# Streaming conformer layer: VectorE's scalings by GpSimd's root, kept behind the VectorE instruction given just ahead of them

## The chip, the core and the metric

The kernel runs on one core of a Trainium2 chip. The metric is device time in microseconds for one launch, the median of several runs. A core has five engines with a queue of instructions each, issued in order: TensorE (matmuls and transposes, PE in the profile), VectorE (DVE), ScalarE (ACT), GpSimd (POOL) and SyncE (SP), whose queue here issues most DMA transfers. Engines wait for each other through semaphores.

## What is computed

One layer over 2048 prompt rows and 64 sample rows of width 1024, in float32:

```
h = rms_norm(x, norm1_g) * (1 + sc1) + sh1
z = h @ w_in
glu_a, glu_b, q, k, v, g_conv, g_attn = split(z)
u = glu_a * sigmoid(glu_b)
conv_out = silu(layer_norm(depthwise_conv31(hist, u) + b_dw)) @ w_conv_out
q = rms_norm(q.reshape(T, 8, 64), q_norm_g)
k = rms_norm(k.reshape(T, 8, 64), k_norm_g)
attn_out = band_attend(q, k, v, rel_bias) @ w_attn_out
x = x + gt1 * ((sigmoid(g_conv) * conv_out + sigmoid(g_attn) * attn_out) @ w_o)
h2 = rms_norm(x, norm2_g) * (1 + sc2) + sh2
x = x + gt2 * ((silu(gate) * up) @ w_ffn_out)
```

`sh1` to `gt2` come from a small product of a condition vector with `w_ada`; `gate` and `up` are the halves of `h2 @ w_ffn_in`. Each row attends to its own chunk of 64 and the eight before it. Returned are the rows, and the last rows of the convolution's input, of k and of v. What matters here are the three norms of the first part: each scales a row (or one head of it) by `1/sqrt(mean(x*x) + eps)`.

## The kernel before

**Stages.** The first part (to about 1,200 us) computes everything up to the mixers' outputs, in four blocks of token rows (576, then 512 each). Per block it runs eight stages: q, k and v, four convolution channel tiles (0 to 3), and the gates g. The second part joins the mixers and runs the feed-forward layers in three blocks. Matmul operands are split into a high and a low part (`whi`/`wlo`, `hh`/`hl`, `part_h`/`part_l`), and each product is three matmuls.

**Who sets the order.** The Python program gives instructions in one order. It keeps an estimate of each engine's load (`Stream`), and side work runs as generators in lanes: `norm_lane` (norms of the next block's rows), `work` (q and k rows), `attn` (attention heads), `tail` (layer norm of the convolution) and `conv` (convolution taps). A generator gives a few instructions, then yields a due time such as `stream.when("pool")`: GpSimd's estimated end less 200 ns. Between the matmuls of the main product, `Stream.tick` lets each lane go on whose due time is past. The framework then orders each engine's queue anew with a model of its own: an instruction that is ready there can go ahead of one that was given earlier and isn't. TensorE is excepted: from the end of the first block's q rows to the end of the first part its order is the given one (`tc.manual_schedule`). A block `with tc.issue_after(ins)` adds, to the instructions given in it on `ins`'s engine, an edge that keeps them behind `ins` in that engine's queue. The edge is order alone; no semaphore is added. The convolution's taps are already held so: each `scalar_tensor_tensor` in `convolve` stays behind the last entry of `ahead_of_taps`, which is the newest softmax step or, in the first block, the newest `t` of q and k rows.

**The norms.** `rsqrt_mean` has VectorE form `t = ssq/count + eps` and GpSimd raise it to the power −0.5 (`r<-t,mhalf` in the profile):

```
dve.tensor_scalar(t[:n, :width], ssq, 1.0 / count, EPS, ALU.mult, ALU.add)
stream.after("pool", "dve")
gps.tensor_tensor(r[:n, :width], t[:n, :width], mhalf[:n, :width], ALU.pow)
```

`qk_rows` runs 34 times, for 17 row tiles of q and 17 of k. ScalarE squares the product and copies it into `kn`; VectorE sums the squares (`ssq<-sq`) and forms `t`; GpSimd takes the root; then, once GpSimd's estimate is past, line 1087 scales `kn` (`kn<-kn,r`, 128x512). For k rows that are returned, a second product `ko<-kn,gk` follows and is stored. 5,000 estimated ns later `store_kq` transposes `kn` on TensorE (four transposes, `pt<-ident,kn`), splits the result on ScalarE (`part_h`) and VectorE (`part_l`) and stores both from SyncE's queue. `part_h` and `part_l` have two buffers each, shared with `conv_norm` and `finish_head`.

`norm_tile` runs 12 times, for the 4 row tiles of blocks 1 to 3. ScalarE sums squares in two halves, VectorE adds them and forms `t`, GpSimd takes the root, and line 1186 scales the rows (`x_t<-x_t,r`, 128x1024). Eight transposes on TensorE follow, in two groups with `h`, `hh` and `hl` made of each.

The first block's five row tiles are scaled elsewhere (`scale_rows`); the change doesn't touch them. The second part has norms of its own, scaled on ScalarE.

**Attention.** In a head, `softmax_max` reads a row tile's scores (`pr<-sc,bias`) on VectorE; the score matmuls of the next row tile (`sc<-kk,q`) wait for it. **Convolution.** `convolve` runs 31 taps over each channel tile, each reading and writing `y`, so that they are a chain on VectorE; for the returned rows it transposes the end of `u` first (`pt<-ident,u`).

Of the kernel before, what the change touches and what calls it, by code (L numbers as in the profile page):

```python
# [11 lines left out]
ALU = mybir.AluOpType  # L12
# [14 lines left out]
NH, HD = 8, 64  # L27
# [595 lines left out]
def streaming_layer(ctx: ExitStack, tc: tile.TileContext, I, O):  # L623
    nc = tc.nc
    stream = Stream()
    pe, dve, act, gps = (
        Meter(e, n, stream) for e, n in ((nc.tensor, "pe"), (nc.vector, "dve"), (nc.scalar, "act"), (nc.gpsimd, "pool"))
    )
# [106 lines left out]
    def either(n, less=0.0):  # L735

        d, p = (max(stream.load[e], stream.load["pe"]) for e in ("dve", "pool"))
        return (gps, "pool") if p + 60 + 2.25 * n + less < d + 75 + 1.04 * n else (dve, "dve")
# [7 lines left out]
    def rsqrt_mean(pool, ssq, n, width, count, bufs=5):  # L746
        t = pool.tile([P, 8], F32, tag="rs_t", bufs=bufs)
        r = pool.tile([P, 8], F32, tag="rs_r", bufs=bufs)
# [3 lines that stand above are left out]
        return r[:n, :width]  # L752
# [30 lines left out]
    def temp(name, shape=(P, 512)):  # L783
        return wk.tile(list(shape), F32, tag="t", name=name, bufs=NT)
# [138 lines left out]
    def first_block(xs):  # L923
# [87 lines left out]
        for i, (t, n) in enumerate(tiles):  # L1011
            for k in (KT - 2, KT - 1):
                product(i, k)
            work.start(qk_rows(pss[i], n, gqk[:, 0:1], q_d, t, None, i > 2))
# [23 lines left out]
    def store_kq(src, n, dst, col, g=None):  # L1038

        pt = ps_g.tile([P, 4, P], F32, tag="gp", name="pt")  # L1040
        for hp in range(4):
            pe.transpose(pt[:, hp, :n], src[:n, hp * P : (hp + 1) * P], ident[:n, :n])
        stream.after("act", "pe")
        hi, lo = parts(shape=(P, 4, P))
        if g is None:
            split(hi[:, :, :n], lo[:, :, :n], pt[:, :, :n])
        else:
            act.activation(hi[:, :, :n], pt[:, :, :n], AF.Copy, scale=g)
            stream.after("dve", "act")
            dve.scalar_tensor_tensor(lo[:, :, :n], pt[:, :, :n], g, hi[:, :, :n].bitcast(F32), ALU.mult, ALU.subtract)  # L1050

        def store():
            for j, t in enumerate((hi, lo)):
                nc.sync.dma_start(dst[j, :, :, col : col + n].rearrange("h p t -> p h t"), t[:, :, :n].bitcast(F32))

        stream.at(stream.when("act", "dve"), store)
# [12 lines left out]
    def qk_rows(ps, n, g, dst, col, out_rows, spare=False):  # L1069
        sq = temp("sq", (P, NH, HD))  # L1070
        ssq = wk.tile([P, NH], F32, tag="ssq8", bufs=5)
        if spare:
            kn = wa.tile([P, 2, NH, HD], F32, tag="x", name="kn", bufs=3)[:, 0]
        else:
            kn = wa.tile([P, NH, HD], F32, tag="kn", bufs=3)
        pv = ps[:n].rearrange("p (h d) -> p h d", h=NH)
        stream.after("act", "pe")
        act.activation(sq[:n], pv, AF.Square)
        act.activation(kn[:n], pv, AF.Copy)
        yield stream.when("act")  # L1080
        dve.tensor_reduce(ssq[:n], sq[:n], AX.X, ALU.add)
        r = rsqrt_mean(wk, ssq[:n], n, NH, HD)
        if col < PBLOCKS[0][1] + (dst is k_d) * CACHE:
            ahead_of_taps.append(dve.last.ins)
        yield stream.when("pool")
        e, name = either(512, TT_LESS)
        e.tensor_tensor(kn[:n], kn[:n], r.unsqueeze(2).to_broadcast([n, NH, HD]), ALU.mult)
        t = stream.when(name)
        if out_rows is not None:
            ko = temp("ko", (P, NH, HD))  # L1090
            e, name = either(512, TT_LESS)
            e.tensor_tensor(ko[:n], kn[:n], gk[:n].unsqueeze(1).to_broadcast([n, NH, HD]), ALU.mult)
            stream.at(stream.when(name), lambda: nc.sync.dma_start(out_rows, ko[:n].rearrange("p h d -> p (h d)")))
        yield t + KN_LAG
        store_kq(kn.rearrange("p h d -> p (h d)"), n, dst, col, g)
# [62 lines left out]
    def square(x_t, n, junk=None):  # L1158
        ssq = wk.tile([P, 2], F32, tag="ssq", name="ssq", bufs=3)
        if junk is not None:  # L1160
            act.activation(junk[:n], x_t[:n], AF.Square, accum_out=ssq[:n, 0:1])
            return rsqrt_mean(wk, ssq[:n, 0:1], n, 1, D)
        for j in range(2):
            act.activation(temp("junk")[:n], x_t[:n, 512 * j : 512 * j + 512], AF.Square, accum_out=ssq[:n, j : j + 1])
        stream.after("dve", "act")
        dve.tensor_tensor(ssq[:n, 0:1], ssq[:n, 0:1], ssq[:n, 1:2], ALU.add)
        return rsqrt_mean(wk, ssq[:n, 0:1], n, 1, D)
# [3 lines left out]
    def load_ahead():  # L1171

        if to_load:
            t = to_load.pop(0)
            ahead_x[t] = load_x(t, P, wa, "x", 3), stream.load["pe"] + X_LAG

    def norm_tile(lo, t, free):

        c = slice(t - lo, t - lo + P)
        while t not in ahead_x:  # L1180
            load_ahead()
        x_t, landed = ahead_x.pop(t)
        yield landed
        r = square(x_t, P)
        yield stream.when("pool")
        dve.tensor_scalar(x_t, x_t, r, None, ALU.mult)
        yield stream.when("dve") + PE_LAG
        for g in range(2):
            pt = ps_g.tile([P, 4, P], F32, tag="gp", name="pt")
            h = temp("h32", (P, 4, P))  # L1190
            for k in range(4):
                pe.transpose(pt[:, k], x_t[:, (4 * g + k) * P : (4 * g + k + 1) * P], ident)
            if g:
                stream.at(stream.when("pe"), load_ahead, True)
            stream.after("dve", "pe")
            for k in range(4):
                kk = 4 * g + k
                dve.tensor_scalar(h[:, k], pt[:, k], A1[:, kk, 0:1], B1[:, kk, 0:1], ALU.mult, ALU.add)
            yield stream.when("dve")
            yield lambda: free["columns"] >= c.stop  # L1200
            f = slice(4 * g, 4 * g + 4)
            act.activation(hh[:, f, c], h, AF.Copy)
            yield stream.when("act")
            dve.tensor_tensor(hl[:, f, c], h, hh[:, f, c].bitcast(F32), ALU.subtract)
    def qkv(b, m, norms):
        lo, hi = PBLOCKS[b]
        tiles = token_tiles(lo, hi)
        ws = {}

        def product(t, n, ps, k):  # L1210
            if k // 2 not in ws:
                ws[k // 2] = W.get(("qkv", m, k // 2))
            wh, wl = ws[k // 2]
            c = slice(t - lo, t - lo + n)
            mm3(ps[:n], hh[:, k, c], hl[:, k, c], wh[:, k % 2], wl[:, k % 2], k == 0, k == KT - 1)
            if (t, n) == tiles[-1] and k % 2:
                W.done()

        for t, n in tiles:
            if t in norms:  # L1220
                norm_lane.drain([norms[t]])
            ps = ps_g.tile([P, 512], F32, tag="gp", name="ps")
            for k in range(KT):
                product(t, n, ps, k)
            if m == 0:
                work.start(qk_rows(ps, n, gqk[:, 0:1], q_d, t, None))
            elif m == 1:
                work.start(qk_rows(ps, n, gqk[:, 1:2], k_d, kcol(t), state_row(ks_p, kn_s, t, n), b == 0 and t > 2 * P))
            else:
                v_rows(ps, n, t)  # L1230
# [415 lines left out]
    for b, stage in ORDER:  # L1646
        lo, hi = PBLOCKS[b]
        if stage == "q":
            free, ahead = {"columns": 0}, {}
            if b + 1 < len(PBLOCKS):  # L1650
                ahead = {t: norm_tile(hi, t, free) for t, _ in token_tiles(*PBLOCKS[b + 1])}
# [728 lines left out]
```

## Time and profile before

| | us |
|---|---|
| median of 3 runs (2952.1 to 2953.67) | 2952.1 |
| profiled execution | 2952.3 |
| its span on the core | 2950.5 |

How to read the profile: a group or a row gives the source line (nearly all have L105, a helper that gives every instruction), the engine, the operation, the written and read tiles with their shapes, and times. In rows in order of time the first number is the start, the second the duration in us, and a bracket at the end gives how long the engine stood idle before the instruction and what ended the wait. Rows of waits read: engine, tile it was about to write, what it waited for, then the sum, the number of times and the longest. PE's granted clock is a share of full speed.

| first part, by stage of time | TensorE busy | VectorE busy | GpSimd busy |
|---|---|---|---|
| 60 to 130 us | 68.34 of 70 | 54.18 | 19.09 |
| 340 to 372 us | 29.99 of 32 | 24.53 | 7.97 |
| 372 to 420 us | 42.30 of 48 | 34.98 | 7.76 |
| 940 to 982 us | 40.09 of 42 | 35.53 | 9.04 |
| 982 to 1230 us | 241.53 of 248 | 169.08 | 43.80 |

### The profile page before, as it was taken

How to read it: one execution, taken by the hardware profiler on the slowest of the kernel's cores; microseconds unless marked ns; L12 is line 12 of the kernel's file. 1: busy time of each engine (PE TensorE's matmuls, PEld its weight loads, DVE VectorE, ACT ScalarE, POOL GpSimd, SP SyncE). 2: the span in 40 equal slices, each digit the busy share in tenths (PEclk: the TensorE clock that was granted, in tenths of full speed). 3: DMA queues.
4: the chain of work that ended last, by engine and by line, in shares of the span. 5: the costliest groups of instructions: out<-in, count | busy, mean ns of one | idle time of the engine just before them, and what ended most of it. 6: DMA issues, size and time to landing. Idle time of an engine off the chain costs nothing.

```text
span 2950.5 us, 44832 instructions
## 1 busy us (share of the span) xinstructions
PE 2890.8 (98%) x16193; PEld 2585.3 (88%) x16193; DVE 2046.4 (69%) x3648; ACT 1363.3 (46%) x2453; POOL 1162.6 (39%) x753
## 2 busy tenths in 40 slices
PE   7999999999999999999999999999999999999999
PEld 5899777887888788888999998999999999999998
DVE  5897788667956885577767746666666557566666
ACT  3345533751465267464334345444444345444442
POOL 1101210111011002454566452366667742465667
PEclk9999999999999999999999999999999999999999
DMA  9989889978995997985444876332333965333333
GB/s 320 316 296 309 279 280 326 295 234 294 290 294 195 308 264 238 282 301 166 143 147 143 277 258 218 96 123 87 114 121 104 337 224 181 97 98 109 115 107 126
DMA packets 467067, 628.04 MB, mean 213 GB/s; under 512 B 36196, under 2 KB 314584, under 8 KB 466845
## 3 DMA queue, kind: packets, MB, share of 16 engines
q1 hardware_dynamic: 452944, 606.11, 63.6%
q10 hardware_dynamic: 13901, 19.08, 1.9%
q8 instruction: 127, 2.08, 0.3%
q14 instruction: 95, 0.78, 0.1%
HBM read 476.53 MB, written 148.54 MB: 212 GB/s over the span
## 4 chain that ended last, share of the span: by engine, by line
PE 46%; DVE 2%; DMA 1%; ACT 1%; issue 1%; POOL 0%; SPq 0%; ACTq 0%; DVEq 0%; POOLq 0%
PE ps L105 28%; PE pd L105 13%; PE pw L105 5%; DVE wlo L105 1%; ACT whi L105 0%; DVE ps L105 0%; DMA cin<-o_d 0%; DMA x<-x_d 0%; DMA wst<-in_w_conv_out 0%; POOL wlo L105 0%; DMA wfo<-in_w_ffn_out 0%; DVE acc L105 0%; DVE sums L105 0%; DVE pw L105 0%; DMA tg<-g_d 0%
## 5 line engine op out<-in xcount | busy, mean ns | idle before, releaser
L105 PE MATMUL ps<-t,whi 128*128 128x384 f32 (+1 forms) x2112 | 501.8, 322 | 3.2 <-DVE u L105 1.1
L105 POOL TENSOR_TENSOR wlo<-wst,whi 128x1024 fp32r<-128x1024 f32 (+1 forms) x159 | 363.4, 2297 | 235.0 <-ACT whi L105 213.6
L105 ACT ACTIVATE whi<-wst 128x1024 fp32r<-128x1024 f32 (+1 forms) x265 | 258.3, 979 | 317.0 <-PE ps L105 127.8
L105 PE MATMUL ps<-b,whi 128*128 128x384 f32 (+1 forms) x1584 | 380.6, 325 | 5.4 <-DVE v L105 2.1
L105 PEld LDWEIGHTS ps<-t,whi 128*128 128x128 f32 x2112 | 367.7, 188 | 10.5 <-ACT u L105 3.3
L105 DVE SCALAR_TENSOR_TENSOR y<-u,wd,y 128x512 f32<-128x512 f32 (+1 forms) x480 | 369.4, 773 | 7.2
L105 PE MATMUL ps<-hh,whi 128*128 128x512 f32 (+2 forms) x992 | 362.6, 365 | 0.1
L105 DVE TENSOR_TENSOR acc<-acc,pd 128x512 f32<-128x512 f32 x482 | 322.0, 684 | 48.4 <-PE pd L105 45.9
L105 PE MATMUL ps<-hh,wlo 128*128 128x512 f32 (+2 forms) x992 | 344.9, 348 | 0.0
L105 PE MATMUL ps<-hl,whi 128*128 128x512 f32 (+2 forms) x992 | 344.3, 347 | 0.0
L105 PE MATMUL ps<-t,wlo 128*128 128x384 f32 (+1 forms) x1056 | 338.2, 321 | 0.0
L105 PE MATMUL pd<-whi,hid 128*128 128x512 f32 x912 | 297.5, 391 | 0.5 <-DVE hid L105 0.3
L105 PEld LDWEIGHTS ps<-b,whi 128*128 128x128 f32 x1584 | 276.8, 188 | 13.6 <-DVE v L105 3.2
L105 ACT ACTIVATE pr<-pr,sm 128x640 f32<-128x640 f32 (+2 forms) x272 | 201.8, 748 | 138.5 <-DVE sm L105 136.6
L105 PE MATMUL ps<-b,wlo 128*128 128x384 f32 (+1 forms) x792 | 256.0, 323 | 0.0
L105 POOL TENSOR_TENSOR r<-t,mhalf 128x1 f32<-128x1 f32 (+2 forms) x68 | 82.3, 1219 | 415.5 <-DVE t L105 383.2
L105 PEld LDWEIGHTS ps<-hh,wlo 128*128 128x128 f32 x992 | 186.4, 188 | 22.7
L105 DVE TENSOR_TENSOR wlo<-wst,whi 128x1024 fp32r<-128x1024 f32 (+1 forms) x106 | 135.6, 1283 | 101.4 <-ACT whi L105 96.8
L105 PEld LDWEIGHTS pd<-whi,hid 128*128 128x128 f32 x912 | 171.1, 188 | 36.9 <-DVE acc L105 1.4
L105 PEld LDWEIGHTS ps<-hh,whi 128*128 128x128 f32 x992 | 187.0, 188 | 18.0 <-issue 2.9
L105 PEld LDWEIGHTS ps<-hl,whi 128*128 128x128 f32 x992 | 187.4, 189 | 14.5 <-issue 1.7
L105 PEld LDWEIGHTS ps<-t,wlo 128*128 128x128 f32 x1056 | 198.1, 188 | 0.8
(233 smaller groups left out, 6299.0 us busy)
## 6 DMA issues: line engine op xcount, KB each, us to landing
whi<-w_din_h SPq DMA_DIRECT2D x72, 512.0 KB, 6.9
wlo<-w_din_l SPq DMA_DIRECT2D x72, 512.0 KB, 7.0
wst<-sum_d SPq DMA_DIRECT2D x131, 256.0 KB, 2.9
wfo<-in_w_ffn_out SPq DMA_DIRECT2D x64, 512.0 KB, 4.1
wmod<-in_w_ada SPq DMA_DIRECT2D x46, 512.0 KB, 9.4
sum_d<-ws SPq DMA_DIRECT2D x88, 256.0 KB, 2.1
wst<-in_w_ffn_in SPq DMA_DIRECT2D x85, 256.0 KB, 3.3
wst<-in_w_in SPq DMA_DIRECT2D x40, 512.0 KB, 6.9
```

The lines of the kernel that those rows point to most:

```text
L105: self.last = f(*args, **kw)
```

## The change

The two scalings are put into a block that keeps them behind `dve.last.ins`, the VectorE instruction given last before them by any lane. Nothing else changes: the same instructions are given in the same order.

```diff
@@ qk_rows
         yield stream.when("pool")
         e, name = either(512, TT_LESS)
-        e.tensor_tensor(kn[:n], kn[:n], r.unsqueeze(2).to_broadcast([n, NH, HD]), ALU.mult)
+        with tc.issue_after(dve.last.ins):
+            e.tensor_tensor(kn[:n], kn[:n], r.unsqueeze(2).to_broadcast([n, NH, HD]), ALU.mult)
@@ norm_tile
         yield stream.when("pool")
-        dve.tensor_scalar(x_t, x_t, r, None, ALU.mult)
+        with tc.issue_after(dve.last.ins):
+            dve.tensor_scalar(x_t, x_t, r, None, ALU.mult)
```

`either(512, TT_LESS)` always chooses VectorE here, since `TT_LESS` is 9e9.

## The prediction

> **What bounds the kernel now.** I read the page's first and fifth parts, then the waits by engine, then the order in time around each scale.
>
> ```profile
> span 2950.5 us, 44832 instructions
> PE 2890.8 (98%) x16193; PEld 2585.3 (88%) x16193; DVE 2046.4 (69%) x3648; ACT 1363.3 (46%) x2453; POOL 1162.6 (39%) x753
> ```
>
> TensorE is busy 98% of the span, so only 59.7 us of it are idle, and the change touches no matmul. A change of VectorE's order can pay only where TensorE stands still for VectorE. The waits by engine say how much that is:
>
> ```profile
> DVE kn L105 <- POOL r L105: 33.4, 25, 3.9
> PE sc L105 <- DVE sm L105: 11.8, 9, 5.7
> ```
>
> VectorE waits 33.4 us in 25 places for GpSimd's root with a scale of `kn` at the head of its queue. TensorE's longest wait, 5.7 us, is that of a score matmul for VectorE's softmax. The first sum is about what VectorE can get back; what reaches the end is the part of it that stands in front of such TensorE waits.
>
> How a scale comes to wait, in VectorE's order in time:
>
> ```profile
> 948.90 0.15 DVE L105 TENSOR_SCALAR t<-ssq 128x8 f32<-128x8 f32 x1
> 949.01 0.75 DVE L105 SCALAR_TENSOR_TENSOR y<-u,wd,y 128x512 f32<-128x512 f32 x1
> 951.29 0.69 DVE L105 TENSOR_TENSOR kn<-kn,r 128x512 f32<-128x512 f32 x1 [1.53 <-POOL r L105]
> 949.20 2.05 POOL L105 TENSOR_TENSOR r<-t,mhalf 128x8 f32<-128x8 f32 x1 [5.87 <-DVE t L105]
> ```
>
> The root starts behind `t` and takes 2.05 us. One convolution tap (0.75) runs under it; then the scale heads the queue and VectorE stands for 1.53 us, though taps that need nothing from elsewhere are queued behind it.
>
> **The change, part by part.** Nothing is added or removed: the same 46 scales (34 of `kn`, 12 of `x_t`) run as long as before. Each may no longer be issued ahead of the VectorE instruction given last before it. By the order in which the kernel gives its instructions, set beside the order of the trace, 37 of the 46 now stand ahead of theirs, by 1 to 40 places; in nine the edge changes nothing. At 951.29 the instruction to be followed is a tap six places on. The root (2.05) is then covered by three taps of 0.75, and the 1.53 goes. What can be late instead is the scale's own reader, four transposes on TensorE, whose order in the first part is fixed by hand. The stores of q and k follow those transposes, so their DMAs on SyncE's queue move only if the transposes stall.
>
> (a) *The score wait at 387.* The order in time of VectorE, GpSimd and TensorE:
>
> ```profile
> 377.70 0.69 DVE L105 TENSOR_TENSOR kn<-kn,r 128x512 f32<-128x512 f32 x1 [0.60 <-POOL r L105]
> 382.21 0.69 DVE L105 TENSOR_TENSOR kn<-kn,r 128x512 f32<-128x512 f32 x1 [0.31 <-POOL r L105]
> 387.27 0.39 PE L105 MATMUL ps<-whi,hl 128*128 128x512 f32 x1
> 388.71 0.69 DVE L105 TENSOR_TENSOR kn<-kn,r 128x512 f32<-128x512 f32 x1 [1.53 <-POOL r L105]
> 389.98 0.68 DVE L105 TENSOR_TENSOR part_l<-o_p,part_h 128x512 fp32r<-128x512 f32 x1
> 393.02 0.27 DVE L105 CUSTOM_DVE_ANT_0 pr<-sc,bias 128x128 f32<-128x128 f32 x1
> 393.35 0.79 PE L105 MATMUL sc<-kk,q 128*128 128x256 f32 x2 [5.70 <-DVE sm L105]
> ```
>
> TensorE has nothing left at 387.66 and waits to 393.35 for the softmax step at 393.02. VectorE reaches that step late, having waited 0.60 + 0.31 + 1.53 = 2.44 us for roots. In the new order the scale of 382.21 comes behind the `part_l` of 389.98, still ahead of the step, and that of 388.71 behind a tap given after the step. Whether the place that it leaves is filled by another tap isn't known, so I count the stalls alone: 2.44. To it comes what the stretch before leaves VectorE ahead, bounded by 0 and 5.66 (the next rows); as VectorE waits there for TensorE and ScalarE too, I take 0.6. The score matmul starts 3.0 us earlier: **−3.0**, bounds 0 and −5.7 (no wait left).
>
> (b) *The stretch before it.*
>
> ```profile
> 346.15 0.69 DVE L105 TENSOR_TENSOR kn<-kn,r 128x512 f32<-128x512 f32 x1 [3.91 <-POOL r L105]
> 349.40 0.69 DVE L105 TENSOR_TENSOR kn<-kn,r 128x512 f32<-128x512 f32 x1 [1.75 <-POOL r L105]
> 355.90 0.51 PE L105 MATMUL sc<-kk,q 128*128 128x256 f32 x2 [0.95 <-DVE sm L105]
> 357.46 0.62 PE L105 MATMUL sc<-kk,q 128*128 128x384 f32 x2 [0.34 <-DVE sm L105]
> 360.67 0.60 PE L105 MATMUL pt<-ident,kn 128*128 128x128 f32 x4
> 366.11 0.74 DVE L105 SCALAR_TENSOR_TENSOR part_l<-pt,gqk,part_h 128x512 fp32r<-128x512 f32 x1
> 363.59 0.69 ACT L105 ACTIVATE part_h<-pt,gqk 128x512 fp32r<-128x512 f32 x1
> ```
>
> The scale of 346.15 has to follow the `part_l` of 366.11, 40 places on, which ends at 366.85. With 3.91 + 1.75 of waits gone and the later scale's 0.69 behind it too, the moved scale ends at 366.85 − 6.35 = 360.5 (its own 0.69 leaves its old place and comes back at the new one). TensorE, without its waits of 0.95 and 0.34, is at the transposes at 359.4: it waits 1.1 there and gets back 1.3. For the end this counts nothing, because the score matmul of (a) is set by VectorE: TensorE comes to it at 387.5 and goes on at 390.35, a wait of 2.9.
>
> (c) *The clock behind that wait.* Windows of VectorE's and TensorE's busy time (columns: PE, PEld, DVE, ACT, POOL busy and instructions; then granted clock, DMA share, GB/s):
>
> ```profile
> 306.79:310.20 3.41, 1.77 (x14) 1.77 (x15) 2.22 (x9) 1.25 (x5) 0.00 (x0) 1.00 0.69 183
> 388.71:392.12 3.41, 0.00 (x0) 0.00 (x0) 3.38 (x6) 0.22 (x1) 0.00 (x0) 1.00 0.65 205
> 392.12:395.53 3.41, 2.18 (x8) 1.89 (x8) 3.41 (x11) 1.30 (x4) 0.00 (x0) 0.50 0.93 269
> 402.00:410.00 8.00, 8.00 (x38) 6.50 (x37) 2.13 (x8) 3.39 (x8) 1.64 (x1) 0.98 1.07 342
> ```
>
> Behind the 3.41 us without a matmul the granted clock is 0.50, until about 402.3 (0.98 over the last row's 8 us leaves 0.3 us at half). From 393.35 that is 9.0 us of matmuls at half speed, 4.5 us lost. The other long wait, which falls into the first row, kept 1.00:
>
> ```profile
> 308.43 0.51 PE L105 MATMUL sc<-kk,q 128*128 128x256 f32 x2 [2.64 <-DVE sm L105]
> ```
>
> The 2.9 of (b) is nearer to 2.64 than to 5.70, so I take the clock as kept: **−4.5**, bounds 0 and −4.5. [...]
>
> (d) *The history transpose at 980.*
>
> ```profile
> 978.27 0.40 PE L105 MATMUL ps<-whi,hl 128*128 128x512 f32 x1
> 979.76 0.68 DVE L105 SCALAR_TENSOR_TENSOR u<-tb,ps 128x512 f32<-128x512 f32 x1
> 980.59 0.27 PE L105 MATMUL pt<-ident,u 128*30 128x128 f32 x1 [1.91 <-DVE u L105]
> ```
>
> VectorE starts `u` at 979.76 although its last input is there at 978.67, because taps are queued ahead. A stall of 1.53 at 951.29 goes in that stretch, and more like it, so the taps are through and `u` starts 1.0 earlier: **−1.0**, bounds 0 and −1.1.
>
> (e) *Late scales elsewhere.*
>
> ```profile
> 96.23 0.68 DVE L105 TENSOR_TENSOR kn<-kn,r 64x512 f32<-64x512 f32 x1 [1.53 <-POOL r L105]
> 102.29 0.69 DVE L105 TENSOR_TENSOR kn<-kn,r 128x512 f32<-128x512 f32 x1 [0.36 <-POOL r L105]
> 107.56 0.60 PE L105 MATMUL pt<-ident,kn 128*128 128x128 f32 x4
> 109.64 0.84 DVE L105 SCALAR_TENSOR_TENSOR y<-u,wd,y 128x606 f32<-128x606 f32 x1
> 125.87 0.63 PE L105 MATMUL pt<-ident,kn 128*128 128x128 f32 x4 [1.66 <-DVE kn L105]
> 128.81 0.69 DVE L105 TENSOR_TENSOR kn<-kn,r 128x512 f32<-128x512 f32 x1 [0.47 <-POOL r L105]
> 130.31 0.60 PE L105 MATMUL pt<-ident,kn 128*128 128x128 f32 x4
> 131.32 0.84 DVE L105 SCALAR_TENSOR_TENSOR y<-u,wd,y 128x606 f32<-128x606 f32 x1
> ```
>
> The scale of 102.29 has to follow the tap of 109.64, which ends at 110.48; less the stalls of 1.53 and 0.36 it ends at 108.6, 1.0 behind its transposes. TensorE then comes 1.0 later to its wait at 125.87, which VectorE sets: it shrinks from 1.66 to 0.66, so 0, bounds −1.7 and +1.0. The scale of 128.81 has to follow the tap of 131.32 (ends at 132.16): less its own 0.47 it ends at 131.7, 1.4 behind the transposes of 130.31. VectorE's lead of 1.53 + 0.36 from before would cover that, if waits between don't eat it: I take the middle, +0.7, bounds 0 and +1.4. Of the others, worked out in the same way, all keep 0.3 us or more; the least are an `x_t` scale and one of `kn`, for which I add +0.3, bounds 0 and +2. Together **+1.0**.
>
> What could take the gain of a covered root away is the root itself: it took 2.05 with one tap under it, and three will run there. [...] No run here shows a root under three taps alone; if it waited for each, the scale would still be behind them in the queue.
>
> Sum: −3.0 − 4.5 − 1.0 + 1.0 = −7.5. The profiled execution took 2952.3 us (span 2950.5 and 1.8 around it), the median of three is 2952.1, so the two can be read as one: 2952.3 − 7.5 = **2944.8**.
>
> **The rivals.**
> 1. *The clock falls all the same.* The wait of 2.9 lies so that the clock drops as at 392.12. Then −4.5 is missing: 2952.3 − 3.0 = 2949.3. For it: the wait is longer than 2.64. Against it: no matmul-free 3.41 us are left.
> 2. *Only VectorE gains.* The stalls go, but the softmax step is not issued sooner, since the taps that fill them are given ahead of it. TensorE's waits stay: 2952.3, give or take 1. For it: VectorE is busy 69% and its idle time is not the bound. Against it: (a) shows a step that TensorE waits for behind a stall.
> 3. *Slower: the scale of 346.15 is held by its late `part_l`.* That `part_l` waits on its part buffers, which earlier stores free, and not on VectorE's place in the queue. If it isn't earlier than 366.11, the scale ends at 366.85 + 0.69 = 367.5, TensorE stands 6.9 at the transposes of 360.67, and the clock falls (10.2 us at half, 5.1 lost). VectorE, in order, stands too, so (a) and (c) bring nothing: +12.0 − 1.3 − 1.0 + 1.0 = +10.7, 2963.0. It decides once this stall and the clock exceed what (a), (c) and (d) give, from about 3.5 us of stall. For it: 40 places are by far the longest move, and ScalarE wrote the `part_h` to it only at 363.59. Against it: that stretch begins with 5.66 us of VectorE waits that go.
>
> **How the numbers follow.** The forecast has 0.45, the fallen clock 0.17, no effect on TensorE 0.10, the held scale (with other late scales, each at its transposes) 0.28. What a measurement here can tell from no change is about 0.2%, 5.9 us. The forecast's own range is 2941 to 2948 (2.7 more in (a), 3 more in (e)); nine tenths of it lie below 2946.2 and a tenth of rival 1: faster 0.42. Slower is rival 3: 0.28. The rest, 0.30, is within. As both signs hold much, the range reaches from 2939 to 2961, which leaves out some 0.05 below and 0.12 above.
>
> **What would show it.** Right, if the wait of `kn` for the root falls from 33.4 to under 15 us with two or more taps between `t` and the scale; if the score wait of 5.70 is under 3.4 and the granted clock stays 1.00 from 380 to 410; if the history transpose waits about 0.9. Wrong, if transposes of `kn` or `x_t` show new waits for VectorE of over 3 us in sum, above all the second `kn` ones after 355; if the clock drops at another place in the first part; or if the span's growth or saving lies behind 1230 us, where no scale is touched.

## The result and the profile after

The changed kernel takes 2943.6 us (median of 6 runs, 2941.3 to 2945.2), the kernel before, measured beside it, 2952.9 (6 runs, 2948.9 to 2957.7). The ratio is 0.9967, 95% interval 0.9957 to 0.9977: 9.3 us less. The profiled execution took 2941.7 us, its span is 2939.5, 11.0 below that of before.

The page of the changed kernel, first part, and its waits by engine (sum, times, longest):

```profile
span 2939.5 us, 44832 instructions
PE 2889.3 (98%) x16193; PEld 2587.5 (88%) x16193; DVE 2053.9 (70%) x3648; ACT 1362.7 (46%) x2453; POOL 1164.9 (40%) x753
...
DVE kn L105 <- POOL r L105: 4.7, 6, 1.8
...
PE pt L105 <- DVE kn L105: 6.1, 2, 4.0
...
PE sc L105 <- DVE sm L105: 2.7, 5, 1.3
```

TensorE's idle time falls from 59.7 to 50.2 us (2939.5 − 2889.3), so 9.5 of the 11.0 us are waits that went. VectorE's wait for the root goes from 33.4 us in 25 places to 4.7 in 6, the score matmuls' wait for the softmax from 11.8 to 2.7. New are two waits of transposes for a late scale (6.1; before there was one of 1.7).

TensorE runs the same 16,193 matmuls in the same order in both traces. So the start of the n-th matmul after, less that of the n-th before, shows place by place where time came from. Negative is sooner:

| time in before | what happens there | step | lag behind it |
|---|---|---|---|
| 107 to 126 | `kn` transposes wait 2.15; the wait of 1.66 at 125.87 is gone | +2.35, −1.86 | 0.0 |
| 308 | the score wait of 2.64 is gone | −2.0 | −1.9 |
| 312 to 345 | small steps | −0.6 | −2.5 |
| 355 to 357 | the waits of 0.95 and 0.34 are gone | −1.75 | −4.3 |
| 360.67 | `kn` transposes wait 3.96 | +4.1 | −0.2 |
| 361 to 370 | half clock (+3.1), a wait of 0.65 gone (−0.9) | +2.2 | +2.1 |
| 393.35 | the score wait of 5.70 is gone | −5.85 | −3.8 |
| 393 to 402 | full clock where it was half | −4.0 | −7.8 |
| 403 | new score wait of 1.25 | +1.5 | −6.3 |
| 470 to 480 | half clock | +1.9 | −4.4 |
| 752 | TensorE's wait of 0.71 for the DMA of `in_w_ada` is gone | −1.0 | −5.9 |
| 858 to 863 | score waits of 0.45 and 0.36 are gone | −1.4 | −7.3 |
| 980 | the history transpose's wait of 1.91 is gone | −2.7 | −10.1 |
| behind 1230 | no scale there | about −0.2 | −10.8 |

Three of these rows are not shown to be the change's. The step at 858 to 863 (−1.3 to −1.4) stands in the trace of every other run below, also of those without an edge there (block 1 alone, and the kernel before with two roots): those two waits belong to the one profiled execution of before. The step at 752 is a wait for a transfer, and it is also gone (−1.0) in the kernel before with two roots, which has no edge at all; in before it reads

```profile
753.81 0.64 PE L105 MATMUL pa<-wmod,cl 128*32 128x256 f32 x8 [0.71 <-DMA wmod<-in_w_ada]
```

And a second profile of the changed kernel has +0.7 at 470 for +1.9.

The order in time of TensorE and VectorE in the changed kernel shows the two places that decide:

```profile
356.16 0.39 PE L105 MATMUL ps<-whi,hl 128*128 128x512 f32 x1
360.51 0.63 PE L105 MATMUL pt<-ident,kn 128*128 128x128 f32 x4 [3.96 <-DVE kn L105]
...
359.02 0.75 DVE L105 SCALAR_TENSOR_TENSOR part_l<-pt,gqk,part_h 128x512 fp32r<-128x512 f32 x1 [1.13 <-ACT part_h L105]
359.68 0.68 DVE L105 TENSOR_TENSOR kn<-kn,r 128x512 f32<-128x512 f32 x1
...
389.21 0.28 DVE L105 CUSTOM_DVE_ANT_0 pr<-sc,bias 128x128 f32<-128x128 f32 x1
```

The scale that stood at 346.15 now follows its `part_l` and ends at 360.36; TensorE has been waiting for it since 356.55. The softmax step that came at 393.02 now comes at 389.21, and TensorE, itself late by then, doesn't wait for it at all.

The windows of the same trace (columns as in the prediction: PE, PEld, DVE, ACT, POOL busy; then granted clock, DMA share, GB/s):

```profile
358.17:361.58 3.41, 1.07 (x7) 1.02 (x8) 1.35 (x2) 0.69 (x1) 0.00 (x0) 1.00 0.92 244
361.58:368.40 6.82, 6.82 (x24) 5.84 (x23) 4.71 (x11) 3.13 (x6) 0.00 (x0) 0.50 1.08 387
372.00:420.00 48.00, 46.75 (x257) 37.45 (x256) 41.62 (x86) 20.21 (x46) 7.33 (x6) 1.00 0.94 279
470.80:474.22 3.42, 3.03 (x14) 1.93 (x15) 0.42 (x1) 0.00 (x0) 0.00 (x0) 0.50 1.03 414
```

The half clock behind 392 is gone, and TensorE's 42.30 busy us between 372 and 420 have become 46.75. But the clock now falls at 361.58, behind the new wait, and again at 470.80. From 30 to 2,900 us both traces have 17.07 us at half clock: 10.24 + 6.83 before (at 392 and 1174), 6.83 + 3.41 + 6.83 after (at 361, 471 and 1174). In these two executions the clock was moved, not won.

### The profile page after: what moved, and what is told of

Same layout as the page of the kernel before. It is cut to its first block, busy times and chain, and to the rows that moved or that the text cites. A ratio compares the mean times of both kernels' runs of the same rounds, so it can differ in the third digit from the quotient of the medians.

```text
span 2939.5 us, 44832 instructions
## 1 busy us (share of the span) xinstructions
PE 2889.3 (98%) x16193; PEld 2587.5 (88%) x16193; DVE 2053.9 (70%) x3648; ACT 1362.7 (46%) x2453; POOL 1164.9 (40%) x753
## 4 chain that ended last, share of the span: by engine, by line
PE 47%; DVE 2%; ACT 1%; DMA 1%; issue 1%; POOL 0%; SPq 0%; ACTq 0%; DVEq 0%; POOLq 0%
PE ps L105 29%; PE pd L105 13%; PE pw L105 5%; DVE wlo L105 1%; ACT whi L105 1%; DVE ps L105 0%; DMA cin<-o_d 0%; DMA x<-x_d 0%; DVE acc L105 0%; ACT xn L105 0%; DMA wst<-in_w_ffn_in 0%; DMA wfo<-in_w_ffn_out 0%; DMA tg<-g_d 0%; DVE sums L105 0%; PE pt L105 0%
## 5 line engine op out<-in xcount | busy, mean ns | idle before, releaser
L105 PEld LDWEIGHTS ps<-t,whi 128*128 128x128 f32 x2112 | 367.8, 188 | 10.1 <-ACT u L105 3.9
L105 ACT ACTIVATE pr<-pr,sm 128x640 f32<-128x640 f32 (+3 forms) x272 | 201.9, 749 | 137.1 <-DVE sm L105 134.8
```

What stands on the lines that cost most here:

```text
L105: self.last = f(*args, **kw)
```

## The experiments

### Which of the two edges

*q and k rows alone:* the edge at line 1087 only.

```diff
-        with tc.issue_after(dve.last.ins):
-            dve.tensor_scalar(x_t, x_t, r, None, ALU.mult)
+        dve.tensor_scalar(x_t, x_t, r, None, ALU.mult)
```

> Only the scaling of q and k rows is held; that of token rows is free as before. If the gain comes from VectorE's waits for the root that stand ahead of a TensorE wait, this part carries most of it: progress of TensorE against before, matmul by matmul, gains about 4 us between 345 and 405 us and about 2.7 at 980; the 2 us at 305 and the 1 us near 860 (both next to token-row scalings) stay away. About 7 us below before, some 2945. If the token rows bring it, this is within 2 us of before, 2951 to 2954. If it was only the place of the clock's windows, the time is anywhere between 2945 and 2957 and the score wait of 5.7 us near 387 is still there.

*Token rows alone:* the edge in `norm_tile` only.

```diff
-        with tc.issue_after(dve.last.ins):
-            e.tensor_tensor(kn[:n], kn[:n], r.unsqueeze(2).to_broadcast([n, NH, HD]), ALU.mult)
+        e.tensor_tensor(kn[:n], kn[:n], r.unsqueeze(2).to_broadcast([n, NH, HD]), ALU.mult)
```

> Only the scaling of token rows is held. By the stalls: the score wait of 2.6 us near 308 goes, some 2 to 3 us are gained up to 330 and about 1 near 860; the score wait of 5.7 near 387 with its half clock stays, and so does the wait of 1.9 at 980. 2949 to 2950. If token rows bring the gain, 2945 or less.

Measured beside each other (before 2954.3): q and k alone 2943.4, ratio 0.9963 (0.9948 to 0.9977); token rows alone 2956.1, ratio 1.0007 (0.9998 to 1.0017). The waits and, for the token rows, TensorE's order in time and a window, of the two runs:

```profile
PE pt L105 <- DVE kn L105: 6.1, 2, 3.9
PE sc L105 <- DVE sm L105: 3.1, 5, 1.2
```

```profile
309.12 0.51 PE L105 MATMUL sc<-kk,q 128*128 128x256 f32 x2 [2.19 <-DVE sm L105]
395.06 0.79 PE L105 MATMUL sc<-kk,q 128*128 128x256 f32 x2 [5.72 <-DVE sm L105]
983.09 0.27 PE L105 MATMUL pt<-ident,u 128*30 128x128 f32 x1 [1.92 <-DVE u L105]
384.00:404.00 20.00, 14.28 (x58) 11.44 (x57) 16.24 (x34) 7.12 (x19) 2.26 (x2) 0.74 0.90 292
```

With q and k alone the waits are those of the whole change. With token rows alone every long wait of before stands, with its half clock. The 2949 to 2950 expected of the token rows did not come. The edge at q and k rows carries all of it, the step at 308 too, which the expectations had given to the token rows.

### Which block

*Block 1 alone* (columns 576 to 1087) and *everything but block 1*, each by a condition on the edge:

```diff
-        with tc.issue_after(dve.last.ins):
+        with tc.issue_after(dve.last.ins) if col >= 576 and col < 1088 and dst is q_d or dst is k_d and 576 + CACHE <= col < 1088 + CACHE else nullcontext():
```

The second has the condition negated and keeps the edge of the token rows; the first has no edge there.

> Only the eight q and k row tiles of block 1 (scaled between 331 and 405 us) are held. By the stalls: the new wait of about 4 us at 356 to 360, the score wait near 387 gone, some 4 us gained up to 405, and the waits at 308 and 980 as before. 2948 to 2949. If the gain at 405 needs the 2 us won at 305 by the token rows, there is 2 us or less here: 2950 to 2952.

> The changed kernel without the edge at the q and k rows of the block of columns 576 to 1087 (block 1); every other scale keeps it. If the gains add up stretch by stretch: block 1's waits come back as before (the score wait of about 5.7 us near 387 and the half clock behind it), the waits of 0.95 and 0.34 near 355 too, no new wait of the kn transposes near 360, and only the steps outside the stretch 320 to 410 stay: about 2.0 at 305 to 308 (if that one belongs to a q or k edge of another block), 1.0 at 752, 1.1 at 858 to 863, 2.7 at 980. That gives about 2952.9 - 6 = 2947, ratio 0.998. Rival: the gain at 980 or at 305 hangs on how far TensorE is ahead, which block 1 set; then less than 3 us are left, about 2950 to 2952, and block 1 with the rest gives more than the sum of the two alone (block 1 alone gave about 1).

Block 1 alone: 2952.1 (before 2954.3), ratio 0.9991 (0.9981 to 1.0001). All but block 1: 2946.3 (before 2953.5), ratio 0.9975 (0.9965 to 0.9985). TensorE's order in time, first block 1 alone (its profiled execution had a span of 2961.4 and a mean granted clock of 0.992, where its nine other executions have 0.994 to 0.997, so its times are shifted), then all but block 1:

```profile
372.41 1.09 PE L105 MATMUL pt<-ident,kn 128*128 128x128 f32 x4 [6.31 <-DVE kn L105]
988.00 0.27 PE L105 MATMUL pt<-ident,u 128*30 128x128 f32 x1 [1.91 <-DVE u L105]
```

```profile
357.35 0.51 PE L105 MATMUL sc<-kk,q 128*128 128x256 f32 x2 [0.99 <-DVE sm L105]
359.34 0.62 PE L105 MATMUL sc<-kk,q 128*128 128x384 f32 x2 [0.80 <-DVE sm L105]
395.57 0.79 PE L105 MATMUL sc<-kk,q 128*128 128x256 f32 x2 [6.03 <-DVE sm L105]
```

The main places divide cleanly. Block 1's edges remove the waits of 355 to 357 and of 393 and bring the one at the `kn` transposes; the steps at 308 (here −2.9 with +1.1 just ahead of it) and 980 (−2.7) are the other blocks'. The sum of the two, 2.2 + 7.2 = 9.4 us, is that of the whole change, within the intervals. Block 1 alone came out next to the second of its two forecasts (2950 to 2952). So the stretch on which the prediction spent most of its words, 340 to 420, brings about 2 us with an interval that reaches to none; the places that it priced at −1.0 or not at all bring the rest. The expectation for all but block 1 (2947, the gains add up) was met.

### Is it the root?

An edge also changes VectorE's order, so the gain might come from another order of the taps and not from the root that is now covered. Here GpSimd takes each q and k root twice, the first into a tile that nobody reads. VectorE's own order stays: by operation and tile all its 3,648 operations come in the same order as without the second root, in before and in the changed kernel; only the root is there about 1.64 us later.

```diff
+        if width == NH:
+            r2 = pool.tile([P, 8], F32, tag="rs_x", bufs=bufs)
+            nc.gpsimd.tensor_tensor(r2[:n, :width], t[:n, :width], mhalf[:n, :width], ALU.pow)
         gps.tensor_tensor(r[:n, :width], t[:n, :width], mhalf[:n, :width], ALU.pow)
```

> The kernel before, with GpSimd taking the root of each q and k row tile twice (the first into a tile that nobody reads), so that each root that a scale waits for comes about 1.64 us later. If in the kernel before the wait for the root stands on VectorE's queue and a part of it reaches TensorE: VectorE's wait of kn for the root grows from 33.4 to 65 to 80 us, the score wait at 387 from 5.7 to 7 to 10, and the time grows by 3 to 15 us, to about 2956 to 2968. Rival (only VectorE's idle time, nothing of it reaches TensorE): the waits grow as much and the time stays within 2 us of before.

> The changed kernel, with GpSimd taking the root of each q and k row tile twice. If the edges have put enough work between t and the scale: the second root of 1.64 us is covered in most places, VectorE's wait for the root stays under 20 us in sum, and the time stays within 2 us of the changed kernel, about 2943 to 2946. Rival (the cover is just enough for one root, or the gain came from another order of the taps and not from the covered root): the wait grows by 25 us or more and TensorE loses as the kernel before does with two roots, 3 us or more, 2947 or higher.

Before with two roots: 2991.5, ratio 1.0122 (1.0102 to 1.0141), 38 us more. The changed kernel with two: 2951.2 (before 2953.5), ratio 0.9985 (0.9974 to 0.9996), 7.6 us above the changed kernel's 2943.6. The page and the waits of the first, then the waits of the second:

```profile
span 2990.2 us, 44852 instructions
PE 2904.9 (97%) x16193; PEld 2595.6 (87%) x16193; DVE 2047.4 (68%) x3648; ACT 1364.0 (46%) x2453; POOL 1219.5 (41%) x787
...
DVE kn L105 <- POOL r L105: 79.6, 29, 5.5
...
PE sc L105 <- DVE sm L105: 22.2, 9, 10.5
PE pt L105 <- DVE part_l L105: 10.4, 3, 7.0
PE pt L105 <- DVE kn L105: 7.4, 4, 4.8
...
PE pt L105 <- DVE u L105: 4.2, 1, 4.2
```

```profile
DVE kn L105 <- POOL r L105: 21.6, 13, 3.3
```

The wait for the root grew by 46.2 us in before, as both theories had it, and the end moved by 38. The rival, that only VectorE's idle time grows, is out by far; but the theory's bound of 15 us was too low as well. TensorE's idle time grew by 25.6 (2990.2 − 2904.9 = 85.3, against 59.7): the places of before with longer waits (score 10.5 for 5.7, history transpose 4.2 for 1.9), and new ones, above all 7.0 us near 86 us. Its busy time grew by 14.1 for the same matmuls, and that goes with the clock, whose mean granted share was 0.988 for 0.996 in the profiled execution of before. A wait for a root was a wait of VectorE's whole queue (the 1.53 us at 951.29 in before, with taps queued behind the scale), and here TensorE paid for most of what was added. The price is not the same in the other direction: the change took 28.7 us of these waits away (33.4 to 4.7) and won some 10.

In the changed kernel the wait grew by 16.9. By matmul, against the changed kernel's profile, its end is 9.5 us later. Of these 2.1 come ahead of 30 us, where no q or k root is; 4.3 between 75 and 85, where the first block's first scales follow each other with no taps to run under a root; 3.5 between 105 and 115, where the late `kn` scale is later still (its transposes wait 4.0 for 2.15, which is 1.85 of it). Behind 115 us the sum is −0.3. So the theory held from the second block on, and its "within 2 us" fell on the first. Its bound of 20 us for the wait was missed too (21.6), and the time lies where the rival had it (2947 or higher), though without the rival's 25 us of added waiting. What these two runs show is that the changed kernel bears a later root where the kernel before doesn't. They don't show that each step of the change comes from a covered root; a run of before with a shorter root, which would, was not made.

### The late scales

The wait of 3.96 near 360 looks like a loss to be had back. *One tile free:* the edge everywhere but at the q tile of column 832, whose scale ended at 360.36.

```diff
-        with tc.issue_after(dve.last.ins):
+        with tc.issue_after(dve.last.ins) if dst is k_d or col != 832 else nullcontext():
             e.tensor_tensor(kn[:n], kn[:n], r.unsqueeze(2).to_broadcast([n, NH, HD]), ALU.mult)
```

> The changed kernel without the edge for one of the 46 scalings, that of the q row tile that has to follow the late low part (346.15 us before, 40 places on). If that one makes TensorE's new wait of 3.96 us and the clock's fall behind it, both go: no half clock between 355 and 370, and 1 to 4 us below the changed kernel, 2939 to 2943. If TensorE only comes sooner to the next wait that VectorE sets, the score wait near 387 grows from nothing to 3 to 5.7 us with the clock's fall behind it, and the time is that of the changed kernel or 3 more, 2943 to 2947.

It took 2940.0 (before 2954.3), ratio 0.9952 (0.9936 to 0.9967): about 3.5 us under the changed kernel. The time was that of the first theory, but the score wait came as in the second (3.78, below). The next run frees the tile of the wait of 2.15 near 109 too (block 0's k tile of token 64): `col != (320 if dst is k_d else 832)`.

> The changed kernel without the edge at two scales, those whose transposes TensorE reached first: the q tile of column 832 (the wait of 4.0 near 360) and block 0's k tile of token 64 (the wait of 2.3 near 107). If a late scale costs what TensorE then waits: no wait of pt for kn over 0.7 us is left, and the time is that of the run with the first tile free alone, less 0 to 2 us: about 2938 to 2940, ratio 0.9945 to 0.995. Rival: the 2.3 of near 107 is only moved, since the wait of 1.66 near 126 comes back with it; then the time is the same as with the first tile free, 2940.

2941.2 (before 2953.5), ratio 0.9946 (0.9929 to 0.9964), no better than with one free. Its `kn` transposes wait 1.9 once, near 130 in place of 107: the rival's reading, a wait that is moved (the rival had 126). As the intervals of all these overlap, the changed kernel and the one with a free tile were set beside each other on one chip, with a third that has q and k edges alone and the same tile free:

> The changed kernel itself, beside the two below on one chip, to compare them with it. 2941 to 2945, ratio to before 0.9955 to 0.998, as before.

> The changed kernel with the q tile of column 832 free, once more on the chip of the changed kernel. If the late scale of that tile cost the end 2 to 4 us: 2938 to 2941.5, at least 2 below the changed kernel, intervals of the ratio that do not meet or hardly. Rival (the 3.5 us seen were the phase of the half-clock windows of one call): within 1.5 us of the changed kernel.

> The edge at q and k rows alone, with the q tile of column 832 free, and no edge at the token rows. If the token rows' edges bring nothing with the others either: the same time as the run with all edges but one, 2938 to 2941.5. Rival (the token rows' edges matter once the others are there): 2 us or more apart from it, either way.

Beside before (2952.2): the changed kernel 2942.95, ratio 0.9966 (0.9954 to 0.9978); one tile free 2942.96, ratio 0.9965 (0.9953 to 0.9976); q and k with one tile free 2941.5, ratio 0.9959 (0.9944 to 0.9973). The gain of 3.5 is gone: no version is shown to beat the changed kernel, and leaving out the token rows' edges makes no difference that these runs can tell. TensorE's order in time in the changed kernel's second profile, then in the first and second profile of the one with a free tile, with two windows of the latter:

```profile
359.48 1.09 PE L105 MATMUL pt<-ident,kn 128*128 128x128 f32 x4 [3.99 <-DVE kn L105]
```

```profile
388.44 0.50 PE L105 MATMUL sc<-kk,q 128*128 128x256 f32 x2 [3.78 <-DVE sm L105]
```

```profile
388.42 0.53 PE L105 MATMUL sc<-kk,q 128*128 128x256 f32 x2 [3.79 <-DVE sm L105]
356.00:388.00 32.00, 27.97 (x156) 22.09 (x144) 30.03 (x59) 14.31 (x31) 6.33 (x4) 1.00 0.92 280
388.80:395.62 6.82, 6.82 (x24) 5.73 (x22) 6.02 (x14) 2.66 (x9) 0.21 (x1) 0.50 1.00 344
```

Without the late scale the wait at 360 is gone and the clock stays full to 388; and there the score wait is back with 3.78, and the half clock behind it. VectorE owes TensorE some 4 us in this stretch, and the edge decides mostly at which of the two places TensorE pays: by matmul the free tile gains 0.9 us between 354 and 405 in its first profile and 1.9 in its second, each against a profile of the changed kernel, and that is less than two executions of one kernel can differ by: the two profiles of the kernel with a free tile agree to 0.1 us in these waits, yet their spans are 2936.9 and 2941.2. By matmul the second loses 1.7 us at 471 to 480, 0.6 near 971, and 1.5 between 1,160 and 1,230, where its longest wait is 3.4 for 1.3; its mean granted clock is 0.996, that of the first 0.998.

## Why the prediction was right, and where it wasn't

The time was right (2944.8 forecast, 2943.6 measured), the sum of its parts less so: −7.5 against −10.8 by matmul, of which −1.4 (858 to 863) is not the change's. Point by point:

- **Covered roots: right.** VectorE's wait for the root fell to 4.7 us, and four taps (948.60 to 951.71 in the changed kernel) run between `t` and the scale that stood for 1.53. The two-root runs show that a later root is paid for by TensorE in the kernel before, and hardly in the changed one behind the first block. What could have taken it back, a root slowed by three taps, did not come here; it took 2.06 us under them, for 2.05 under one in before:

```profile
948.60 3.11 DVE L105 SCALAR_TENSOR_TENSOR y<-u,wd,y 128x512 f32<-128x512 f32 x4
951.63 0.68 DVE L105 TENSOR_TENSOR kn<-kn,r 128x512 f32<-128x512 f32 x1
948.79 2.06 POOL L105 TENSOR_TENSOR r<-t,mhalf 128x8 f32<-128x8 f32 x1 [5.00 <-DVE t L105]
```

- **(a) right, a little small.** The score matmul at 393.35 was to be 3.0 sooner and is 3.8 sooner.
- **(b) the step that was mis-sized.** "It waits 1.1 there" is 3.96. The scale's end was right (360.36 for 360.5); TensorE's arrival was not: 356.55 for 359.4. The prediction moved TensorE by the waits of its own stretch, 1.3, and left out what it had gained upstream: 2.0 at 308, 0.6 to 345, and 1.75 in place of 1.3. With the 2.15 near 107 the late scales cost 6.1 of waits, twice the 3 that the prediction had named as a sign of being wrong. "For the end this counts nothing" holds for the wait, as far as the free tile shows: without it, the same is paid at 388.
- **(c) right at its place, by another way, and given back elsewhere.** Behind 393 the clock stays full (1.00 from 372 to 420), −4.0 for −4.5. The wait of 2.9 that was to be short enough did not occur, since TensorE itself came late; that 2.9 would have kept the clock is not shown, and in another run the clock was 0.50 behind a wait of 2.15 (last section). Here the outcome was luck. And behind the 3.96 the clock fell to 0.50 at 361.58 (+3.1 up to 368), which the prediction had named as a sign of being wrong and had given to its third rival alone; and 1.9 went at 470 to 480. Over these two traces the clock term is 0 (17.07 us at half in both).
- **(d) mis-sized.** −2.7 for −1.0, with bounds of 0 and −1.1. The step "its last input is there at 978.67" was wrong: 978.67 is the end of TensorE's work ahead of the transpose, and those matmuls belong to another product. The last matmul that `u` waits for ends near 975.5 in before, so `u` was 4 us late behind the queued taps, not 1.1; in the changed kernel it is formed at 968.13, 0.26 us behind the matmul that it waits for, and the transposes wait for nothing.

```profile
968.13 0.69 DVE L105 SCALAR_TENSOR_TENSOR u<-tb,ps 128x512 f32<-128x512 f32 x1 [0.26 <-PE ps L105]
971.03 0.27 PE L105 MATMUL pt<-ident,u 128*30 128x128 f32 x1
```

- **(e) right at 107 to 126**, where the late scale's wait (2.15 for 1.0) was got back at 125.87 to within 0.1 us; the +0.7 at 130 and the +0.3 did not come.
- **Not foreseen: 308**, −2.0 (752 and 858 to 863, −2.4 together, weren't either, but are not shown to be the change's). At 308 no scale of `kn` is near (the next is at 331), and the edges of the `x_t` scales at 290 and 313 alone leave the wait (2.19). VectorE's order shows what happened: in before four `y<-y,pm` additions, from 303.79 on, stand ahead of the softmax step at 308.07; in the changed kernel all four stand behind it. In before the first of them and the step; then the same stretch in the changed kernel:

```profile
303.79 0.68 DVE L105 TENSOR_TENSOR y<-y,pm 128x512 f32<-128x512 f32 x1
...
308.07 0.29 DVE L105 CUSTOM_DVE_ANT_0 pr<-sc,bias 128x128 f32<-128x128 f32 x1 [0.25 <-DMA bias<-rb_d]
```

```profile
304.69 0.29 DVE L105 CUSTOM_DVE_ANT_0 pr<-sc,bias 128x128 f32<-128x128 f32 x1 [0.16 <-DMA bias<-rb_d]
...
304.90 0.68 DVE L105 TENSOR_TENSOR y<-y,pm 128x512 f32<-128x512 f32 x1
...
305.64 1.86 DVE L105 TENSOR_TENSOR y<-y,pm 128x512 f32<-128x512 f32 x3
```

  None of these has one of the new edges. The runs show that the step comes with the q and k edges outside block 1. That the framework's model, which orders by its own times, picks differently once the scales ahead have moved is the reading; it was not tested by itself. So these 2 us come with another order of VectorE's instructions, not with a covered root at that place.
- **The rivals.** That TensorE gains nothing is out. The clock that falls all the same did fall, at another place. The held scale had its mechanism in part: the `part_l` at 359.02 waited 1.13 for a `part_h` that had itself waited 1.10 for the store to free its buffer. But it came 7.1 us sooner than before, not unmoved; and beside each other on one chip the kernels with and without the 3.96 took the same time.

By place: up to 410 us −6.5 was forecast (a, c and e) and −6.3 came. The gains at 308 and 355 and the larger loss at 360 with its half clock all end at the score matmul of 393, so that their errors show there as 0.8. Behind 410 us −1.0 was forecast (d) and −4.5 came, which is why the profiled time lies below the forecast; but of that −1.4 is not the change's, and for the +1.9 of half clock at 471 the changed kernel's second profile has +0.7. So that the sum came so near is in part luck: up to 410 the +1.0 of (e) that did not come is made up for by a new score wait of +1.5 at 403, and behind it (d) was too small.

## What to carry to other kernels

Where an engine waits in its own queue for a short instruction of another, as VectorE here for the root (33.4 us in 25 places), what stands behind it waits too; to see whether it matters, double the short instruction and look at the end (here 46 us more of VectorE's waiting, 38 us more in all). What it costs to lengthen the wait is not what is won by removing it: 28.7 us less of it won some 10. To tell whether a moved instruction is late, shift both it and its reader: the reader comes sooner by all that the change gains upstream, not only nearby. And with a clock that falls to half for 3.41 to 10.24 us at a time, as here, a difference of a few us between two kernels counts only when repeated on one chip: 3.5 us under the changed kernel on one chip was 0.0 when the two were measured beside each other. A step that the change is said to bring should also be missing in the runs without the edge: 1.4 us of the table above is not.

## What the runs showed of the hardware

From 30 to 2,900 us the half clock (0.50) lasted 10.24 and 6.83 us in before, and 6.83, 3.41 and 6.83 in the changed kernel: one to three times 3.41. Within each of these two traces the falls lie on one grid of such steps: in before at 392.12 and 229 steps later, in the changed kernel at 361.58, and 32 and 238 steps later. The same wait of 2.15 of the block 0 transposes left the clock at 1.00 in the changed kernel, where it runs over an edge of the grid (107.25 to 109.40), and had 0.50 behind it in the run with q and k edges alone, where one step holds all of it (3.41 less 1.26 busy). That its place in the grid makes the difference is a reading of these two; it was not tested. Two steps of the grid, first of the one, then of the other:

```profile
105.57:108.98 3.41, 1.67 (x8) 1.03 (x6) 3.15 (x5) 2.78 (x5) 0.00 (x0) 1.00 0.55 155
108.98:112.40 3.42, 3.00 (x15) 2.57 (x16) 3.42 (x6) 1.64 (x2) 0.00 (x0) 1.00 0.91 298
```

```profile
107.48:110.89 3.41, 1.26 (x8) 0.85 (x7) 3.41 (x6) 1.84 (x3) 0.00 (x0) 1.00 0.88 269
110.89:114.30 3.41, 3.41 (x9) 2.65 (x9) 3.41 (x5) 1.62 (x2) 0.00 (x0) 0.50 0.92 304
```

With TensorE busy for 1.67 of 3.41 us the clock stayed at 1.00, behind 1.26 it was 0.50. It was 0.50 too behind the 1.07 of the window from 358.17 to 361.58. So a wait of 2.15 us was not safe, where the prediction took 2.9 to be. And behind the same wait of 3.96 to 3.99 the half clock lasted 6.83 us in one execution of the changed kernel and 10.2 in another. The windows of the second, ahead of the clock's fall and behind it:

```profile
354.70:358.10 3.40, 0.79 (x3) 0.30 (x3) 1.88 (x4) 2.08 (x4) 0.00 (x0) 1.00 0.74 174
358.10:368.30 10.20, 8.82 (x29) 7.68 (x30) 5.98 (x13) 3.13 (x6) 0.00 (x0) 0.50 1.02 363
```

How long TensorE was busy does not sort these windows by itself. Of the changed kernel, the window ahead of the fall at 470.80:

```profile
467.39:470.80 3.41, 1.75 (x24) 0.32 (x16) 2.29 (x5) 1.63 (x3) 0.67 (x1) 1.00 1.06 398
```

Behind these 1.75 us of short matmuls the clock was 0.50 (470.80 to 474.22); behind the 1.67 above, and behind the 1.77 of the prediction's first window, it stayed at 1.00. What decides it was not tried.
